# All of the squared-ReLU MLP's down projection as seven block products, with four moves around it

## The chip, the cores and the metric

The kernel runs on one core of a Trainium2 chip. The metric is the device time of one launch in microseconds (us), lower is better. TensorE (PE), VectorE (DVE), ScalarE (ACT), GpSimd (POOL) and SyncE (SP) run their own instruction streams and wait for each other by semaphores. SP issues nearly all loads, POOL most stores to scratch memory and every DMA that adds into its destination. Everything is in float32.

## What is computed

One layer of a streaming encoder, for 512 prompt frames and 32 sample frames taken together as T = 544 columns, with D = 2048:

```python
y, conv, k, v, logf = parallel_mixer(rmsnorm(x, g_mix), ...)      # gated conv ++ forgetting attention, w_in and w_out
x = x + y
x = x + cross_attention(rmsnorm(x, g_xattn), mk, mv, w_xq, w_xo)
x = x + square(relu(rmsnorm(x, g_mlp) @ w_up)) @ w_down           # hidden 8192
out = rmsnorm(x, g_final)
```

The gain of an RMS norm is put on the input of the projection that follows; the reciprocal root of the mean square (`rstd`) is a factor for each column, and is multiplied on the projection's output. So a projection's matmuls need not wait for the norm, but whatever takes its output does.

## The kernel before

**The arithmetic.** Activations lie transposed, a tile is 128 features x 544 columns (halves of TH = 272). A float32 operand is split into a rounded part and a rest: ACT copies it to `whi` (L84), DVE subtracts (`wlo`, L85), and a product takes three matmuls (hi·hi, hi·lo, lo·hi) of 128x128 weights by 272 columns. The large projections use a block scheme with seven products for a 2x2 block product instead of eight (class `Seven` for the input and up projections, with names b11, t1, t2, b22, t3, b21, t4): sums of weight blocks (`s1` to `s4`, tiles `sum`) and of activation blocks ("forms") are multiplied, and the results go to three PSUM areas (`mmx`, `mmy`, `mmz`). One "pair" is two output tiles, 7 products of 24 matmuls, 168 in all.

**The order.** The stages follow each other in program order: head (the first four input tiles, `w_first`), input projection by pairs, attention, output projection, cross-attention, its output projection with the residual tiles x3, up projection (32 pairs), down projection, final norm. A scheduler places each engine's instructions by the order in which they are written; `tc.high_priority(offset=AHEAD)` moves the splits and sums of weights ahead. Every engine then runs its own list in order: one that waits holds up all behind it.

**Buffers.** A pool tag with `bufs=n` is a ring: a tile waits until the one n before it is released. `raw` (3) and `raw2` (4 in the up projection) hold loaded weight blocks, `tmp` (6) holds passing tiles. Slots A, B, C of 16 tiles each hold the forms of the activations (t1/t2, b21/b22, t3/t4 in that order), later the down projection's forms 0 to 3 (A and B) and the residual x3 (C).

**Around the change.** The head sums the squares of x on DVE (`square`, L187), and `rb = rstd(acc_x, D, early=150)` is made before the first pair. The residual's squares go to `acc<-sq`, DMAs that add into two accumulators `acc_3` (L1085 to L1086); a chain of seven for each, each waiting for the one before. Their tiles `sq` are in the `raw2` ring except the last. The first up pair makes `rb_3` from them (matmuls `ssq`, L178), between t2 and b22.

The hidden layer has 64 tiles of 128. Tiles 4 to 59 (56 of 64) go as seven block products: 28 pairs leave `forms` in scratch memory (`fd`), and seven chunks of four pairs by eight output pairs p (L1251) run 7 products of 12 matmuls each. The first four and the last four tiles are plain: `hd`, `w_ends`, a stage of 384 matmuls (L1238) ahead of the chunks and another (L1327) behind them, the latter in two halves of columns, so that the first half's norm and the stores of its output (L1333) go beside the second half's matmuls. During the stage ahead SP loads the first chunk's forms.

Of the kernel before, what the change touches and what calls it, by code (L numbers as in the profile page):

```python
# [8 lines left out]
F32 = mybir.dt.float32  # L9
# [6 lines left out]
D = 2048  # L16
# [13 lines left out]
CH = 8  # L30
# [7 lines left out]
NF = 28  # L38
# [3 lines left out]
def hybrid_step(  # L42
# [3 lines left out]
    w_in, w_first, w_f, w_out, w_xq, w_xk, w_xv, w_xo, w_up, w_dn, w_ends,  # L46
# [9 lines left out]
    tpool = ctx.enter_context(tc.tile_pool(name="tmp", bufs=6))  # L56
# [111 lines left out]
    def rstd(acc, dim, width=T, early=0):  # L168
        accs = acc if isinstance(acc, list) else [acc]
        with tc.high_priority(offset=early):  # L170
            rt = npool.tile([128, T], F32, tag="rstd", name="rstd", bufs=3)
# [21 lines left out]
    wf = cpool.tile([128, KD, 8], F32, name="wf")  # L193
    wf_hl = cpool.tile([128, KD, 16], F32R, name="wf_hl")
# [128 lines left out]
    def seven(pl, ops, ws, out, scale, mid, prefetch, between=None, late=0):  # L323
# [12 lines left out]
        s.b22()  # L336
        s.t3()
# [13 lines left out]
    acc_x = new_acc()  # L351
# [3 lines left out]
    headp = head_cm.__enter__()  # L355
    heads = [mm_tile(), mm_tile()]
# [3 lines left out]
    for j in range(8):  # L360
        xr = [headp.tile([128, T], F32, tag="xr", name="xr", bufs=5) for i in range(2)]
        for i in range(2):
            sp.dma_start(xr[i], xT[j + 8 * i])
        hi, lo = weights(w_first[j])
        x = headp.tile([128, 4, TH], F32, tag="x", name="x", bufs=2)
        for i in range(2):
            act.activation(x[:, 2 * i:2 * i + 2], two(xr[i]), AF.Identity, scale=gain(G_MIX, j + 8 * i))
# [12 lines left out]
        for i in range(2):  # L380
            square(xr[i], acc_x, j + i == 0)
    head_cm.__exit__(None, None, None)
    act.dma_start(wf, w_f)
    split(wf_hl[:, :, 0:8], wf_hl[:, :, 8:16], wf)
# [14 lines left out]
    rb = rstd(acc_x, D, early=150)  # L399
    rbs = npool.tile([128, T], F32, tag="rstd", name="rbs", bufs=3)  # L400
    dve.tensor_scalar(rbs, rb, SCALE, None, ALU.mult)
# [151 lines left out]
    steps = (lambda: gate_open(z16), gate_exp, gate_log, gate_close, gate_sum, turn_logf)  # L553
    ps = emit_logf()
    nxt = fetch_pair(0)
    for t, (n, j) in enumerate((("hr", 0), ("gc", 0), ("gb", 0), ("hr", 1))):
        dve.tensor_tensor(first_tiles[t], first_tiles[t], rb, ALU.mult)
        kinds[n][1](j, first_tiles[t])
    z16 = evac_logf(ps)
    held = []  # L560

    def release():
        while held:
            held.pop()()

# [15 lines left out]
    for i in range(last):  # L581
# [3 lines left out]
        nxt = seven(pj, xops, nxt, out, scale, mid, ahead, release, 2 if i == 0 else 0)  # L585
        done(i, out[1])
        if i < len(steps):
            steps[i]()
        if pairs[i][1] == ("gb", 7):
            release()  # L590
# [833 lines left out]
```

## Time and profile before

| | |
|---|---|
| median of 3 runs | 2350.08 us (2349.14 to 2350.31) |
| profiled execution, its own time | 2352.74 us |
| its span | 2351.0 us (so 1.7 us lie around the span) |
| PE busy | 2312.8 us, 98%, 18151 matmuls |
| DVE busy | 1999.7 us, 85% |
| ACT / POOL busy | 1300.0 us, 55% / 212.2 us, 9% |
| DMA | 420.25 MB, mean 179 GB/s |

A matmul's record is longer (about 288 ns) than the distance to the next, since matmuls overlap; the pace is read from how many start in a stretch. In a row of the timeline, "x4" are records run together, and the bracket holds the idle time just before and what ended it. "PEclk" is the granted clock as a share of the full one.

### The profile page before, as it was taken

To read this page: it belongs to the slowest core of one execution; us is meant where nothing else is said; L and a number is where in the kernel's file an instruction comes from. 1 tells how busy PE (TensorE), PEld (TensorE's weight loads), DVE (VectorE), ACT (ScalarE), POOL (GpSimd) and SP (SyncE) were. 2 spreads that over 40 slices of the span, in tenths; PEclk is the share of its full clock that TensorE was granted. 3 is DMA by queue.
4 is the path that set the end of the run, shared out by engine and by line. 5 is a ranking of instruction groups with operands and counts; after the bars stand their busy time and mean duration, and the time that the engine had idled before them with its cause. 6 is when DMAs were issued, how large, how long until landed. Compare 5 with 4: busy or idle time off the path is not lost.

```text
span 2351.0 us, 47516 instructions
## 1 busy us (share of the span) xinstructions
PE 2312.8 (98%) x18151; PEld 2285.0 (97%) x18151; DVE 1999.7 (85%) x3546; ACT 1300.0 (55%) x2524; POOL 212.2 (9%) x402
## 2 busy tenths in 40 slices
PE   8999999999999999899999999999999999999997
PEld 8999999999999998799999999999999999999997
DVE  9999988877767757889999999998598888888887
ACT  8455555555644546556666566665255555555555
POOL 0000011114200001111111111111000000000000
PEclk9999999999999999999999999999999999999999
DMA  5333345578435537656565566556946636645523
GB/s 177 127 121 122 122 156 160 160 243 300 141 100 154 157 107 212 200 162 204 191 199 180 193 201 196 188 185 226 344 148 241 211 125 233 228 141 191 184 90 131
DMA packets 161861, 420.25 MB, mean 179 GB/s; under 512 B 19096, under 2 KB 23888, under 8 KB 161632
## 3 DMA queue, kind: packets, MB, share of 16 engines
q1 hardware_dynamic: 109888, 313.54, 39.8%
q0 software_dynamic: 46240, 94.75, 13.1%
q10 hardware_dynamic: 5504, 8.93, 1.1%
q8 instruction: 142, 2.33, 0.4%
q14 instruction: 87, 0.71, 0.1%
HBM read 319.91 MB, written 93.33 MB: 176 GB/s over the span
## 4 chain that ended last, share of the span: by engine, by line
PE 94%; DMA 2%; DVE 2%; ACT 1%; issue 1%; DVEq 0%; ACTq 0%; SPq 0%; POOLq 0%
PE mmx L271 27%; PE dx L1233 14%; PE mmy L271 14%; PE mm L120 13%; PE mm L1233 11%; PE mmz L271 7%; PE mm L1327 2%; PE mm L378 1%; PE h L378 1%; PE mm L914 1%; PE s L644 1%; DMA acc<-sq 1%; DMA raw<-in_w_ends 1%; DVE wlo L85 1%; DMA f<-fd 1%
## 5 line engine op out<-in xcount | busy, mean ns | idle before, releaser
L84 ACT ACTIVATE whi<-raw 128x512 fp32r<-128x512 f32 x664 | 417.8, 631 | 493.9 <-PE mmx L271 97.9
L84 ACT ACTIVATE whi<-sum 128x512 fp32r<-128x512 f32 x652 | 407.5, 630 | 418.6 <-PE mmx L271 186.2
L85 DVE TENSOR_TENSOR wlo<-raw,whi 128x512 fp32r<-128x512 f32 x664 | 453.3, 687 | 129.2 <-ACT whi L84 121.6
L85 DVE TENSOR_TENSOR wlo<-sum,whi 128x512 fp32r<-128x512 f32 x652 | 436.7, 684 | 70.3 <-ACT whi L84 65.9
L271 PE MATMUL mmx<-oph,whi 128*128 128x272 f32 x1296 | 372.8, 288 | 2.3 <-ACT h L280 2.2
L271 PE MATMUL mmx<-oph,wlo 128*128 128x272 f32 x1296 | 374.0, 289 | 0.1
L271 PE MATMUL mmx<-opl,whi 128*128 128x272 f32 x1296 | 371.5, 287 | 0.0
L1233 PE MATMUL dx<-f,whi 128*128 128x272 f32 x1792 | 344.4, 288 | 0.0
L1233 PEld LDWEIGHTS dx<-f,whi 128*128 128x128 f32 x1792 | 281.5, 188 | 0.0
L1233 PE MATMUL mm<-f,whi 128*128 128x272 f32 x1344 | 258.6, 288 | 0.0
L1233 PE MATMUL dx<-f,wlo 128*128 128x272 f32 x896 | 258.4, 288 | 0.0
L271 PE MATMUL mmy<-oph,whi 128*128 128x272 f32 x864 | 249.8, 289 | 7.6 <-ACT whi L84 7.6
L271 PE MATMUL mmy<-oph,wlo 128*128 128x272 f32 x864 | 249.9, 289 | 0.0
L271 PE MATMUL mmy<-opl,whi 128*128 128x272 f32 x864 | 248.9, 288 | 0.0
L271 PEld LDWEIGHTS mmx<-oph,whi 128*128 128x128 f32 x1296 | 244.0, 188 | 3.1 <-ACT h L280 2.6
L271 PEld LDWEIGHTS mmx<-oph,wlo 128*128 128x128 f32 x1296 | 243.3, 188 | 0.5 <-DVE wlo L85 0.5
L271 PEld LDWEIGHTS mmx<-opl,whi 128*128 128x128 f32 x1296 | 243.5, 188 | 0.0
L1233 PEld LDWEIGHTS mm<-f,whi 128*128 128x128 f32 x1344 | 210.6, 188 | 0.0
L1233 PE MATMUL mm<-f,wlo 128*128 128x272 f32 x672 | 193.4, 288 | 0.0
L271 PEld LDWEIGHTS mmy<-oph,whi 128*128 128x128 f32 x864 | 163.4, 189 | 8.1 <-ACT whi L84 8.0
L1233 PEld LDWEIGHTS dx<-f,wlo 128*128 128x128 f32 x896 | 168.9, 189 | 0.0
L271 PE MATMUL mmx<-b,whi 128*128 128x272 f32 x864 | 166.1, 289 | 0.1
(393 smaller groups left out, 5161.5 us busy)
## 6 DMA issues: line engine op xcount, KB each, us to landing
raw<-in_w_up SPq DMA_DIRECT2D x128, 512.0 KB, 3.9
raw<-in_w_dn SPq DMA_DIRECT2D x112, 512.0 KB, 4.4
f<-fd SPq DMA_DIRECT2D x196, 272.0 KB, 5.7
fd<-form POOLq DMA_DIRECT2D x168, 272.0 KB, 4.2
raw<-in_w_in SPq DMA_DIRECT2D x88, 512.0 KB, 3.8
raw<-in_w_out SPq DMA_DIRECT2D x32, 512.0 KB, 4.2
raw<-in_w_ends SPq DMA_DIRECT2D x20, 512.0 KB, 4.2
kq<-hl POOLq DMA_DIRECT2D x32, 256.0 KB, 3.3
```

The costliest lines, as they stand in the source:

```text
L84: act.activation(hi, src, AF.Copy)
L85: dve.tensor_tensor(lo, src, hi.bitcast(F32), ALU.subtract)
L120: pe.matmul(ps[a], w, two(x)[:, a], start=first and n == 0, stop=last and n == 2)
L271: pe.matmul(ps, a[:, c], x, start=first and j == 0 and n == 0, stop=j == 7 and n == 2, skip_group_check=not first)
L378: pe.matmul(ps[a], w[:, c], xs[a][q], start=j + i == 0 and n == 0, stop=j + i == 8 and n == 2)
L644: pe.matmul(s[:, :N], q[a][:, c], k[b][:, :N], start=n == 0, stop=n == 2)
L914: pe.matmul(ps[:, 0, :NMEM], w[:, c], x, start=k == 0 and n == 0, stop=k == KD - 1 and n == 2)
L1233: pe.matmul(ps, a[:, c], f[:, x], start=first and j == 0 and n == 0, stop=j == 3 and n == 2, skip_group_check=not first)
L1327: pe.matmul(ps, w[:, c], two(x)[:, a], start=k == 0 and j == 0, stop=k == 3 and j == 2)
```

## The change

1. All 64 hidden tiles go as block products: `NF` is 32 pairs instead of 28, the chunks are eight, `hd` and `w_ends` are gone. The last p of the last chunk is plain in two halves of columns, 96 matmuls (`ws`, `hs`; forms b12 of the last chunk are kept in `bd`); for it the final norm's squares go to POOL's adding DMAs (`complete`), and after it there are two `last_rstd`; the first half's eight stores follow the first of these.
2. The last two up pairs run in step (`fourteen`, product by product of both), and their forms are made in parts behind p = 1 to 6 of the first down chunk.
3. The first chunk's forms are loaded directly behind the last weights of the up projection, into slots A, B as they come free; new pools release their buffers tile by tile.
4. Residual's squares of j > 4 go to `tmp` (7 buffers instead of 6), and `rb_3` is written behind b22 (`behind`).
5. Head: the first weights are loaded ahead of x, its squares go to adding DMAs, and `rb`, its products with the first four tiles and their convolution move into the first input pair (`begin`). The pool `keep` closes later and a few sample tiles come from `tmp`.

```diff
-NF = 28
+NF = 4 * CH
-    tpool = ctx.enter_context(tc.tile_pool(name="tmp", bufs=6))
+    tpool = ctx.enter_context(tc.tile_pool(name="tmp", bufs=7))
...
-    def seven(pl, ops, ws, out, scale, mid, prefetch, between=None, late=0):
+    def seven(pl, ops, ws, out, scale, mid, prefetch, between=None, late=0, behind=None):
...
         s.b22()
+        if behind:
+            behind()
         s.t3()
...
+        if j == 0:
+            hi, lo = weights(w_first[j])
         for i in range(2):
             sp.dma_start(xr[i], xT[j + 8 * i])
-        hi, lo = weights(w_first[j])
+        if j:
+            hi, lo = weights(w_first[j])
...
         for i in range(2):
-            square(xr[i], acc_x, j + i == 0)
+            if j:
+                sq = tmp("sq")[:, :T]
+                act.activation(sq, xr[i], AF.Square)
+                pool.dma_start(acc_x[i], sq, accum_op=ALU.add)
+            else:
+                act.activation(acc_x[i], xr[i], AF.Square)
...
-    rb = rstd(acc_x, D, early=150)
...
+    def begin():
+        rstd(acc_x, D, out=rb)
+        for t, (n, j) in enumerate((("hr", 0), ("gc", 0), ("gb", 0), ("hr", 1))):
+            dve.tensor_tensor(first_tiles[t], first_tiles[t], rb, ALU.mult)
+            kinds[n][1](j, first_tiles[t])
+        box["z"] = evac_logf(ps)
+        dve.tensor_scalar(rbs, rb, SCALE, None, ALU.mult)
...
-        nxt = seven(pj, xops, nxt, out, scale, mid, ahead, release, 2 if i == 0 else 0)
+        nxt = seven(pj, xops, nxt, out, scale, mid, ahead, release if i else begin, 0 if i else 2)
...
-            sq = (tmp("sq") if j == 7 else up.tile([128, 1024], F32, tag="raw2", name="sq", bufs=4))[:, :T]
+            sq = (tmp("sq") if j > 4 else up.tile([128, 1024], F32, tag="raw2", name="sq", bufs=4))[:, :T]
...
-    for i in range(4 * CH):
+    for i in range(NF - 2):
         h1, h2 = tmp("h1")[:, :T], tmp("h2")[:, :T]
...
+        nxt = seven(up, ops, nxt, (h1, h2), (relu, relu), square_mid, ahead, None, 0 if i else 2,
+                    None if i else (lambda: rb_3.append(rstd(acc_3, D))))
+        square_mid(h2)
+        forms(i, h1, h2)
+    ss = [Seven(up, ops, ws, (tmp("h1")[:, :T], tmp("h2")[:, :T]), (relu, relu), square_mid, True) for ws in nxt]
+    fourteen(ss)
+    parts = []
+    for k, s in enumerate(ss):
+        square_mid(s.out[1])
+        parts += forms_in_parts(NF - 2 + k, *s.out)
...
+    fs = {f: load_form(0, f) for f in (5, 6, 0, 1)}
+    first = dweights(0, 0)
+    fs.update({f: load_form(0, f) for f in (2, 3)})
+    load_x3(0)
+    fs[4] = load_form(0, 4)
...
+        for p in range(8 if c < NF // 4 - 1 else 7):
...
+            if c == 0 and 1 <= p <= len(parts):
+                parts[p - 1]()
+            if c == NF // 4 - 1:
+                complete(p)
...
+            if a:
+                if i == 0:
+                    rb_4 = last_rstd(sums[0])
+                for p in range(4 * i, 4 * i + 4):
+                    store(p, 0, finish((0, p), rb_4, dve))
+    rb_4 = last_rstd(sums[1])
+    rb_5 = tmp("rb")[:, :TH]
+    act.activation(rb_5, rb_4, AF.Copy)
     for p in range(8):
-        store(p, 1, finish((1, p), rb_4))
+        store(p, 1, finish((1, p), rb_5 if p in (2, 4, 7) else rb_4, pool if p in (2, 4, 7) else dve))
```

What this does to the lists of instructions, at three places. PE in the first up pair, where the matmuls `ssq` of the residual's norm stand (`inv_88` is the matrix of 1/D; `mmx`, `mmy` with `b`, `oph`, `opl` are the pair's own products b11 and t1). Before, behind 23 matmuls of the pair:

```order
L271 MATMUL mmx<-b_12760,whi 128x272 x2
L271 MATMUL mmx<-b_12760,wlo 128x272
L271 MATMUL mmy<-oph,whi 128x272
L271 MATMUL mmy<-opl,whi 128x272
L178 MATMUL ssq<-acc,inv_88 128x272 x2
L271 MATMUL mmy<-oph,wlo 128x272
L271 MATMUL mmy<-oph,whi 128x272
```

And after:

```order
L269 MATMUL mmx<-b_12880,whi 128x272 x2
L269 MATMUL mmx<-b_12880,wlo 128x272
L269 MATMUL mmy<-oph,whi 128x272
L269 MATMUL mmy<-opl,whi 128x272
L269 MATMUL mmy<-oph,wlo 128x272
L178 MATMUL ssq<-acc,inv_88 128x272 x2
L269 MATMUL mmy<-oph,whi 128x272
L178 MATMUL ssq<-acc,inv_88 128x272 x2
L269 MATMUL mmy<-opl,whi 128x272
```

The first `ssq` moved from behind the pair's 23rd matmul to behind its 45th: still inside t1, and not behind b22, where it is written.

DVE in the first input pair, where the first tiles (`hr0`, `gc0`, `gb0`, `hr1`) take the norm's factor (`rstd_900` before, `rb_897` after). Before, between the sums and splits of the pair's first weights, ahead of the split of s2:

```order
L557 TENSOR_TENSOR hr0_888<-hr0_888,rstd_900 128x544
L85 TENSOR_TENSOR wlo_1153<-sum_1089,whi_1152 128x512
L557 TENSOR_TENSOR gc0_889<-gc0_889,rstd_900 128x544
L85 TENSOR_TENSOR wlo_1157<-sum_1089,whi_1156 128x512
L502 TENSOR_TENSOR u_1093<-gc0_889,hr0_888 128x512
```

And after, between the splits of a12 (`raw_1066`) and of a22 (`raw2_1064`), which is the pair's last product, t4:

```order
L85 TENSOR_TENSOR wlo_1299<-raw_1066,whi_1298 128x512
L579 TENSOR_TENSOR hr0_885<-hr0_885,rb_897 128x544
L579 TENSOR_TENSOR gc0_886<-gc0_886,rb_897 128x544
L579 TENSOR_TENSOR gb0_887<-gb0_887,rb_897 128x544
L514 TENSOR_TENSOR u_1201<-gc0_886,hr0_885 128x512
L515 TENSOR_TENSOR u_1201<-gc0_886,hr0_885 128x32
L579 TENSOR_TENSOR hr1_888<-hr1_888,rb_897 128x544
L518 COPY newc_976<-u_1201 128x2
L519 COPY newc_976<-u_1201 128x2
L522 TENSOR_SCALAR y_1208<-u_1201,vec_78 128x546
L582 TENSOR_SCALAR rbs_898<-rb_897 128x544
```

Here a run of unbroken work on the first tiles stands ahead of one split, where before it alternated with splits a pair earlier.

SP between the up and the down projection (`f` with `fd` are the chunk's forms, `x` with `x3d` the residual, `in_w_up`, `in_w_dn` and `in_w_ends` the weights). Before:

```order
L222 DMA raw<-in_w_up 128x1024
L93 DMA raw<-in_w_ends 128x1024 x2
L1193 DMA hh<-hd_0_11795 128x544
L1193 DMA hl<-hd_1_11796 128x544
L1193 DMA hh<-hd_0_11797 128x544
```

And after, from the last form 3 of the first chunk to the weights of p = 1:

```order
L1247 DMA f_21946<-fd_3_11822 128x544
L1247 DMA f_22097<-fd_0_11826 128x544
L1247 DMA f_22099<-fd_0_11833 128x544
L1247 DMA f_22101<-fd_0_11840 128x544
L1247 DMA f_21952<-fd_4_11802 128x544
L1247 DMA f_21954<-fd_4_11809 128x544
L1247 DMA f_21956<-fd_4_11816 128x544
L1282 DMA x_21948<-x3d_11778 128x544
L1282 DMA x_21950<-x3d_11779 128x544
L1247 DMA f_21958<-fd_4_11823 128x544
L1282 DMA x_21960<-x3d_11780 128x544
L1282 DMA x_21962<-x3d_11781 128x544
```

The plain stage's loads are gone. The 28 form tiles of the first chunk stand directly behind the up projection's weights, three forms of the second chunk among them, and the last form 4 stands behind two residual tiles that go to slots C.

More of the change, by code (lines that the diff above doesn't have):

```diff
@@ L1137, in hybrid_step @@
         xo_done(order[i], ps)
-    def plain(m, h):
-        f = ring("form")
-        hi, lo = (f[:, n].rearrange("p a b -> p (a b)") for n in range(2))
-        split(hi, lo, h)
-        pool.dma_start(hd[m][0], hi)
-        pool.dma_start(hd[m][1], lo)
     def forms(i, h1, h2):
@@ L1234, in dproduct, with load_x3 @@
                           skip_group_check=not first)
-    hs = load_hidden(0)
-    fs = [load_form(0, 0), load_form(0, 1)]
-    for p in range(8):
-        hi, lo = weights(w_ends[0, p])
+    def load_x3(p):
         for m in (2 * p, 2 * p + 1):
```

255 lines of the change are left out of this document (139 added, 116 removed).

## The prediction

> **What bounds the kernel now.** I read the page first: the shares of the engines, then the chain that ended last.
>
> ```profile
> span 2351.0 us, 47516 instructions
> PE 2312.8 (98%) x18151; PEld 2285.0 (97%) x18151; DVE 1999.7 (85%) x3546; ACT 1300.0 (55%) x2524; POOL 212.2 (9%) x402
> ...
> PE 94%; DMA 2%; DVE 2%; ACT 1%; issue 1%; DVEq 0%; ACTq 0%; SPq 0%; POOLq 0%
> ```
>
> PE is the bound nearly throughout; a change gains by fewer matmuls or by closing one of PE's few gaps, and loses where it makes another engine late. Next, stretches: near the start, around the first up pair, in the up projection, in the plain stage, in the chunks, in the last plain stage.
>
> ```profile
> core 0: us, PE busy (x) PEld busy (x) DVE busy (x) ACT busy (x) POOL busy (x), PEclk, DMA share, GB/s
> 60.00:100.00 40.00, 38.51 (x302) 34.99 (x300) 37.80 (x72) 17.04 (x34) 1.22 (x2) 1.00 0.35 121
> 100.00:300.00 200.00, 199.20 (x1586) 198.60 (x1586) 188.10 (x325) 103.50 (x187) 10.04 (x19) 1.00 0.37 121
> 955.00:976.00 21.00, 11.15 (x60) 9.41 (x58) 12.19 (x19) 8.17 (x16) 1.72 (x2) 0.76 0.78 221
> 960.00:970.00 10.00, 2.50 (x7) 1.83 (x7) 7.75 (x12) 3.33 (x6) 1.72 (x2) 0.59 0.86 230
> 1000.00:1600.00 600.00, 600.00 (x4785) 600.00 (x4785) 558.28 (x902) 365.16 (x679) 101.59 (x193) 1.00 0.59 191
> 1640.00:1660.00 20.00, 20.00 (x160) 19.99 (x160) 11.13 (x18) 6.30 (x12) 2.12 (x4) 1.00 1.05 361
> 1700.00:2280.00 580.00, 580.00 (x4623) 580.00 (x4623) 508.89 (x877) 306.31 (x606) 0.00 (x0) 1.00 0.53 181
> 2285.00:2336.00 51.00, 49.57 (x388) 48.59 (x386) 43.49 (x97) 37.56 (x85) 0.00 (x0) 1.00 0.41 135
> ```
>
> Steady stages have no gap: 600 us / 4785 matmuls = 0.1254 us each. DVE is at 93 to 94% in the pairs (558.28/600; 188.1/200), so what is added to it there has 6% of room. Only one stretch is bad: 21 us around 965 hold 60 matmuls where 168 fit. What PE waited for, in sums:
>
> ```profile
> PE mmy L271 <- ACT whi L84: 7.6, 2, 6.3
> PE mm L378 <- ACT whi L84: 7.1, 1, 7.1
> PE ssq L178 <- DMA acc<-sq: 3.4, 1, 3.4
> PE mmx L271 <- ACT h L280: 2.2, 2, 1.5
> PE mm L1327 <- DVE x L1329: 1.1, 1, 1.1
> ```
>
> The 7.1 are the kernel's start; 7.6 and 3.4 lie in the first up pair; the 1.1 lies in the last plain stage.
>
> **The change part by part.**
>
> *Matmuls.* Per output pair, seven products of 12 = 84 replace 96. Before: 384 + 384 + 7·8·84 = 5472 in the down projection. After: 63·84 + 96 = 5388. 84 fewer at 0.1254 us: **−10.5 us**, all on the path.
>
> *First up pair.*
>
> ```profile
> 955.04 0.41 PE L271 MATMUL mmx<-b,whi 128*128 128x272 f32 x2
> ...
> 964.15 0.60 PE L271 MATMUL mmy<-oph,whi 128*128 128x272 f32 x1 [6.30 <-ACT whi L84]
> ...
> 968.33 2.18 PE L178 MATMUL ssq<-acc,inv 128*128 128x272 f32 x4 [3.35 <-DMA acc<-sq]
> ...
> 970.76 0.43 PE L271 MATMUL mmy<-opl,whi 128*128 128x272 f32 x1
> 970.99 0.43 PE L271 MATMUL mmy<-oph,wlo 128*128 128x272 f32 x1
> ...
> 974.21 1.08 PE L178 MATMUL ssq<-acc,inv 128*128 128x272 f32 x4
> ...
> 977.17 0.39 PE L271 MATMUL mmy<-oph,whi 128*128 128x272 f32 x1 [1.27 <-ACT whi L84]
> ...
> 1646.33 0.42 PE L120 MATMUL mm<-hl,whi 128*128 128x272 f32 x2
> ```
>
> From 955.04 to 1646.33 are 691.3 us, against 32·168·0.1254 = 674.2 for the 32 pairs: the first one loses 17.1 (the later ones have no gap). Three waits are 10.9 of it, `ssq` 3.3, and the rest the slow pace after the idling: 0.23 us from one matmul to the next at 970.76, clock 0.59. The chain behind both waits is that of the adding DMAs:
>
> ```profile
> 952.09 0.86 POOL L1086 DMA_DIRECT2D acc<-sq  x1 [5.08 <-ACT sq L1085]
> ...
> 961.09 0.86 POOL L1086 DMA_DIRECT2D acc<-sq  x1 [6.13 <-DMA acc<-sq]
> 962.77 0.86 POOL L1086 DMA_DIRECT2D acc<-sq  x1 [0.82 <-DMA acc<-sq]
> ...
> DMA to landing us min/median/max: 4.0/6.7/8.2
> ```
>
> The squares hold `raw2` until their addition has landed, and the first pair's a21, a22 are loaded into that ring; so s1, its split and the 6.30 wait come out of it. With j > 4 in `tmp`, a21 and a22 wait only for j = 3's additions, and the 6.30 wait goes. What is late next is the accumulator itself: the last additions are issued at 961.09 and 962.77 and land some 7 us later, 968 to 970, whatever buffer they come from. In the order after, `ssq` stands behind 45 matmuls of the pair, so PE reaches it at 955.04 + 45·0.1254 = 960.7. Loss after: 960.7 to about 969.6 for wait and first `ssq` 8.9, second `ssq` 1.1, and some 4 us at 0.23 instead of 0.125, 1.8: 11.8. Gain 17.1 − 11.8 = **−5.3**. Bounds: no gain (chain 5 us later, since the weights now load beside it) and −12 (its last links take the 4.0 minimum).
>
> The Trainium skill, page "TensorE: Matmul & The Clock Gate", Part 1: The HAM clock gate, says that an idle window of about 3.4 us halves the clock and that about as much sustained work restores it. The rows agree (0.23 against 0.125 after 6.30 idle), and by it the wait that I leave in would again be followed by a half-rate stretch, as in my 1.8 us; were the wait under 3.4 us, that term would be nil.
>
> *Start.* The first weights now come ahead of x, and DVE scales the first x. Both rows needed for the first matmul (7.09) stay in the same chain of one load, a scaling and splits; bounds −0.7 and +0.8 (one ACT pass over 544 columns less or one more). I take **+0.4**, nearer the extra one, since ACT now copies two weights first. The DVE additions of x's squares (15 of about 0.64) leave the head, which PE bounds with 384 matmuls: nothing.
>
> *`begin`.* The rows of before:
>
> ```profile
> 66.34 0.71 DVE L557 TENSOR_TENSOR hr<-hr,rstd 128x544 f32<-128x544 f32 x1
> ...
> 75.80 0.78 DVE L88 SCALAR_TENSOR_TENSOR ych<-gb,vec,ych 128x544 fp32r<-128x544 f32 x1
> ...
> 77.48 2.48 DVE L85 TENSOR_TENSOR wlo<-sum,whi 128x512 fp32r<-128x512 f32 x4
> ```
>
> The first tiles' work stands between 66.34 and 77.48, 11.1 us, of which some 3.5 are splits and sums of weights: 7.6, and with rstd and rbs about 11 us of DVE. It is now late in the first pair, in an unbroken run of about 6 us ahead of a22's split. A product of 24 matmuls gives 3.0 us of cover, so t4 waits about 2.4 us, and the next pair's first splits about 1.4 twice; with the room of 6% DVE has caught up some 20 us later. Stalls of about 6 in place of those from 60 to 310 (1.5 at 77.45 among them, 3.3 to 4.3 in all): **+2.5**, bounds −1 (the wait at 77.45 gone, splits ahead in time) and +6 (no old stall saved). Four `ssq` in the pair instead of two at the head, at 0.54 (1.08 for two above): **+1.1**.
>
> *Up to down.* At 1640 to 1660 DMA moved 361 GB/s beside 384 plain matmuls (48 us): that cover is gone, and 28 form tiles of 272 KB, 7.6 MB, must land earlier. Slots A come free when t2 of the last two pairs ends, 24 us before the up projection does, slots B 12 us before; the 2.2 MB of each take 6 us at 361 GB/s. Form 4, x3 and the weights of p = 1 (2.3 MB more) compete at the boundary: stall 0 to 3. The forms in parts add about 1.6 us of DVE to p = 1 to 6, on 508.89/580, so 9.2 of the 10.5 that a p takes: a slight overload. Together **+1.5**, bounds 0 and +6 (two MB of 361 GB/s uncovered).
>
> *End.* The last stage runs from 2285 to 2335.7, 50.7 us for 384·0.1254 = 48.1; that 2.6 goes, and four `ssq` of the first half's norm come into the last 96 matmuls, 2.2: **−0.4**. Behind the last matmul:
>
> ```profile
> 2335.74 0.44 DVE L1329 TENSOR_TENSOR x<-x,mm 128x272 f32<-128x272 f32 x1
> ...
> 2337.23 0.72 PE L178 MATMUL ssq<-acc,inv 128*128 128x272 f32 x2 [1.53 <-DVE acc L163]
> ...
> 2340.74 5.17 DVE L1290 TENSOR_TENSOR yout<-yout,rstd 128x544 f32<-128x544 f32 x8
> ```
>
> 15.3 us to the end. After: five of the eight products on DVE (3.2 instead of 5.17, −2.0), one step less in the norm (−0.45), but the first half's products on DVE ahead of the last addition (four of 0.65, up to +2.6) and eight more stores at the very end, 2.2 MB that were spread over 24 us. **+0.5**, bounds −2 and +6 (those 2.2 MB at 361 GB/s). No row shows POOL in such a product. The Trainium skill, page "GPSIMD Engine Reference", section Elementwise — side-by-side cycle accounting, finds two-input elementwise work there about half as fast as on DVE; by that its three would take an estimated 3.9 us against DVE's 3.2 for five, about even.
>
> Sum: −10.5 − 5.3 + 0.4 + 2.5 + 1.1 + 1.5 − 0.4 + 0.5 = −10.2. The profiled execution's 2352.74 would be 2342.5; the median lies 2.66 below it, so **2340.0 us**.
>
> **The rivals.**
>
> *A. The chain of additions stays the whole loss.* The weights' loads move into 943 to 952, where the chain's last links run; DMA share is already 0.78 to 0.86. If each of the last two links lands 2 to 3 us later, the gain of 5.3 is gone: 2345.3, on the border of no change. For it: links took up to 8.2 under load. Against: the bytes are the same, only earlier.
>
> *B. The chain is quick.* Without raw2's block, additions could be issued as squares are made (last at 957), and with 4-us links land near 961: all but the `ssq` themselves and a little goes, −12 instead of −5.3: 2333. Against: POOL's rows at 961.09 wait for the previous addition, not for a buffer.
>
> *C. Slower: the down projection starts dry.* If the forms of the last two-pair stretch don't get through before the boundary (weights and six stored forms for each pair share the queues), 21 of 28 tiles, 5.8 MB, and 2.1 MB of weights come after it: 7.9 MB / 361 GB/s = 22 us, less the 3 to 10 that p = 0 covers: a stall of 12 to 19. It decides from 1.5 + 10.2 + 4.7 = 16 us of stall on; at 19, 2357. Against: the order has the loads directly behind the last weights, and slots A come free 24 us ahead.
>
> *D. DVE does not catch up.* At 94% load, a backlog of 6 us is worked off at 0.06 us per us only, 100 us, and every pair pays some of it: bounded by the backlog, +6 to +8 in place of +2.5: 2345.
>
> **How the numbers follow.** The forecast 0.52, A 0.16, B 0.13, D 0.10, C 0.09. A measurement can tell a change from none at about 0.2%, 4.7 us: below 2345.4 is faster, over 2354.8 slower. Faster: the forecast (0.50 of it), B, and some 0.08 each of A and 0.06 of D: 0.77. Slower: C's upper half and mishaps behind A, 0.06. The rest is the same, 0.17. The range reaches to B below, with the bounds of tail and start added (2329), and to A, D and half of C above (2350).
>
> **What would show it.** Right: 84 fewer down matmuls and chunks of 10.5 us each p; no wait for `whi` near 964, but one for the accumulator of 6 to 9 us at about 5.7 us into the first up pair, followed by matmuls 0.23 us apart; stalls on `wlo` in the first pair's t4; under 3 us of idle PE where up turns into down. Wrong: a wait over 10 us at that boundary, gaps that repeat pair by pair after 100 us, or more than 20 us from the last matmul to the end.

## The result and the profile after

The kernel became slower: 2367.29 us median of 4 runs (2366.63 to 2368.40) against 2350.19 (2349.14 to 2352.57, 4 runs) on the same chip, a ratio of 1.0068 [1.0056, 1.0081], 17 us. The forecast was 2340.0. The head of the page, then stretches as in the prediction (same columns): near the start, around the first up pair, the start of the down projection, its chunks, its last matmuls.

```profile
span 2364.9 us, 47573 instructions
PE 2310.9 (98%) x18083; PEld 2281.7 (96%) x18083; DVE 2008.1 (85%) x3562; ACT 1317.8 (56%) x2569; POOL 246.8 (10%) x447
```

```profile
60.00:100.00 40.00, 37.21 (x279) 34.42 (x280) 31.02 (x60) 15.63 (x31) 1.11 (x2) 0.96 0.30 102
950.00:960.00 10.00, 10.00 (x82) 10.00 (x82) 8.35 (x16) 5.95 (x11) 1.74 (x2) 1.00 1.05 318
960.00:970.00 10.00, 5.79 (x28) 5.25 (x27) 7.51 (x13) 7.38 (x13) 2.26 (x3) 0.66 1.03 309
1650.00:1740.00 90.00, 76.50 (x577) 75.40 (x576) 71.94 (x135) 42.35 (x90) 7.43 (x14) 0.96 0.71 249
1740.00:2280.00 540.00, 539.84 (x4304) 539.62 (x4303) 475.55 (x821) 288.30 (x572) 0.34 (x1) 1.00 0.56 193
2285.00:2347.00 62.00, 61.49 (x480) 60.51 (x479) 43.11 (x77) 41.12 (x87) 8.60 (x10) 1.00 0.41 97
```

PE executes 68 matmuls fewer: 84 products less, 16 `ssq` more (46 instead of 30). The chunks run without a gap (540 us / 4304 = 0.1255 us each). But 1650 to 1740, the first 90 us of the down projection, hold 577 matmuls where 90 / 0.1254 = 718 fit: some 17 us are lost there alone. The first up pair now begins 6 us later, at 960.86, and is still bad (28 matmuls in 960 to 970, before 7). From there to 1649.30 are 688.4 us, 14.3 more than the 674.2 that the prediction counts for 32 pairs.

Cut at four points that both traces have (the first `mm<-yah` of the output projection's second half, the first product of the down projection, its last plain matmul, the end of the span):

| stretch | before, us | after, us | change | foretold |
|---|---|---|---|---|
| start, input projection, attention | 692.79 | 698.79 | +6.0 | +4.0 |
| from there through the up projection | 952.54 | 950.51 | −2.0 | −5.3 |
| down projection to the last plain matmul | 690.09 | 697.53 | +7.4 | −9.4 |
| last plain matmul to the end | 15.6 | 18.1 | +2.5 | +0.5 |
| span | 2351.0 | 2364.9 | +13.9 | −10.2 |

What PE waited for after the change, in sums over the execution (total, times, longest):

```profile
PE mm L386 <- ACT b L84: 8.2, 1, 8.2
PE dx L1276 <- ACT e L1350: 7.9, 8, 3.3
PE dx L1276 <- ACT e L1360: 6.4, 2, 4.4
```

Rows two and three are new: the products of the down projection wait until ACT has copied an earlier product (`e`) out of PSUM. ACT is at 42.35 of 90 us there, so it isn't overloaded; something holds it. ACT's own waits in 1645 to 1735 name it, then a stretch of ACT's timeline, and PE's:

```profile
ACT fp L84 <- DMA fd<-fp: 19.4, 7, 6.0
```

```profile
1654.46 0.38 ACT L1355 ACTIVATE e<-dx 128x272 f32<-128x272 f32 x1
1660.78 0.43 ACT L84 ACTIVATE fp<-acc 128x272 fp32r<-128x272 f32 x1 [5.95 <-DMA fd<-fp]
...
1662.49 0.38 ACT L1360 ACTIVATE e<-dx 128x272 f32<-128x272 f32 x1
```

```profile
1662.92 0.82 PE L1276 MATMUL dx<-f,whi 128*128 128x272 f32 x2 [4.45 <-ACT e L1360]
...
1671.43 0.51 PE L1276 MATMUL dx<-f,whi 128*128 128x272 f32 x2 [2.23 <-ACT e L1350]
```

The forms in parts (`put` in `forms_in_parts`) take their tile `fp` from a ring of three. ACT's rounding copy into a fourth piece must wait until the store of the first has landed. The pieces are written behind p = 1 and later, but the scheduler placed them from the last up pairs on (the first copy starts at 1637.0). Around L1360 of p = 0 ACT's list, with its program names, reads

```
L1355 ACTIVATE e_21966<-dx 128x272
L84 ACTIVATE fp<-acc 128x272 x2
L1360 ACTIVATE e_21967<-dx 128x272
L84 ACTIVATE fp<-acc 128x272
L84 ACTIVATE whi<-raw 128x512
L84 ACTIVATE whi<-sum 128x512 x2
L84 ACTIVATE fp<-h_21400 128x272 x2
```

five pieces in nine instructions, and a ring of three. The first of them waits 5.95 us, the copy `e` at L1360 stands behind it on ACT, and PE, which needs the PSUM area that `e` empties, waits 4.45 and then goes at half rate (0.23 us from one matmul to the next until 1666). The stores themselves are slow there; the answer on the tile `fp` in 1635 to 1740 says

```profile
DMA to landing us min/median/max: 2.3/5.9/8.3
```

### The profile page after: what moved, and what is told of

Its sections match the earlier page's. It is cut to its first block, busy times and chain, and to the rows that moved or that the text cites. A ratio compares the mean times of both kernels' runs of the same rounds, so it can differ in the third digit from the quotient of the medians.

```text
span 2364.9 us, 47573 instructions
## 1 busy us (share of the span) xinstructions
PE 2310.9 (98%) x18083; PEld 2281.7 (96%) x18083; DVE 2008.1 (85%) x3562; ACT 1317.8 (56%) x2569; POOL 246.8 (10%) x447
## 5 line engine op out<-in xcount | busy, mean ns | idle before, releaser
L84 ACT ACTIVATE whi<-sum 128x512 fp32r<-128x512 f32 x676 | 422.4, 630 | 416.5 <-PE mmx L269 186.2
L85 DVE TENSOR_TENSOR wlo<-sum,whi 128x512 fp32r<-128x512 f32 x676 | 453.1, 686 | 88.1 <-ACT whi L84 85.3
L1276 PE MATMUL dx<-f,whi 128*128 128x272 f32 x2016 | 389.6, 289 | 14.3 <-ACT e L1350 7.9
L1276 PEld LDWEIGHTS dx<-f,whi 128*128 128x128 f32 x2016 | 317.6, 189 | 16.5 <-ACT e L1350 9.7
L1276 PE MATMUL mm<-f,whi 128*128 128x272 f32 x1512 | 292.1, 288 | 0.0
L1276 PE MATMUL dx<-f,wlo 128*128 128x272 f32 x1008 | 291.3, 289 | 0.0
L1276 PEld LDWEIGHTS mm<-f,whi 128*128 128x128 f32 x1512 | 238.2, 189 | 0.0
L1276 PE MATMUL mm<-f,wlo 128*128 128x272 f32 x756 | 218.1, 289 | 0.0
L1276 PEld LDWEIGHTS dx<-f,wlo 128*128 128x128 f32 x1008 | 190.6, 189 | 0.0
```

The source lines that it names most:

```text
L84: act.activation(hi, src, AF.Copy)
L85: dve.tensor_tensor(lo, src, hi.bitcast(F32), ALU.subtract)
L1276: pe.matmul(ps, a[:, c], f[:, x], start=first and j == 0 and n == 0, stop=j == 3 and n == 2, skip_group_check=not first)
```

## The experiments

Each kernel was timed against the kernel before on its own chip (medians; ratio with its 95% interval). The edits are against the changed kernel. Theory R is the ring just described; its rivals are that the pieces' work on ACT and DVE, or the traffic of forms, stores and weights at the boundary, is what PE waits for.

### The ring, without its stores

```diff
             split(two(f)[:, 0], two(f)[:, 1], x)
-            pool.dma_start(dst, f)
...
-            sp.dma_start(t.bitcast(F32), fd[4 * c + j][f].bitcast(F32))
+            i = 4 * c + j
+            sp.dma_start(t.bitcast(F32), fd[i if i < NF - 2 else i - 2][f].bitcast(F32))
```

> The changed kernel without the 16 stores of the forms that are made in parts (fp to fd and bd); the last chunk reads older pairs' forms in their place, so the output is not the reference's. The splits on ACT and DVE stay. Theory R (ring): ACT's copy into fp waits for one of 3 buffers that a store still holds (19.4 us of ACT idle on fd<-fp), the copies e of the down products stand behind it on ACT, and PE waits for them. Then the five PE gaps between 1655 and 1730 (13.5 us) and the half-rate stretches behind them go: from the last up matmul to the last plain matmul 697.7 becomes 678 to 681 us, time about 2348 to 2350. Theory W (work): 1.6 us of added DVE and ACT work for each p is too much; the work is unchanged, so the gaps stay within 2 us and the time is 2365 to 2367. Theory D (DMA): the loads of the second chunk saturate the queues and starve the first; only 4.4 MB of stores less, so at least 9 us of gaps stay, 2361 or more.

Measured: 2349.11 against 2351.18, 0.9995 [0.9986, 1.0005]. The down projection takes 680.43 instead of 697.53. The 90 us again:

```profile
1650.00:1740.00 90.00, 89.56 (x714) 89.34 (x713) 86.19 (x161) 52.04 (x107) 0.00 (x0) 1.00 0.73 261
```

714 matmuls instead of 577, with as many copies and subtractions, and no lower DMA share (0.73 against 0.71). So the work of the pieces isn't what PE pays for. The stores' own traffic is gone with them here; the next kernel keeps it.

### The same with every store kept

```diff
-            split(two(f)[:, 0], two(f)[:, 1], x)
+            hi, lo = two(f)[:, 0], two(f)[:, 1]
+            tc.keep_in_program_order(act.activation(hi, x, AF.Copy))
+            dve.tensor_tensor(lo, x, hi.bitcast(F32), ALU.subtract)
             pool.dma_start(dst, f)
...
+    def part(c, p):
+        if c + p and parts:
+            parts.pop(0)()
...
-            if c == 0 and 1 <= p <= len(parts):
-                parts[p - 1]()
+            part(c, p)
```

`part` is called at three places of each p, one piece at a time, and the copy may not be moved ahead of where it is written.

> The changed kernel, all stores kept, three buffers as before, but the 16 pieces of forms are written one at a time (two or three for each p from p = 1 on) and ACT's copy of each is pinned behind what is written ahead of it, so that no two of four wait in a row. Theory R: a piece needs its buffer only 13 us after the one before the last two, a store lands in 2 to 8, so ACT does not wait on fd<-fp; the gaps after the up projection go as without stores: last up matmul to last plain matmul 679 to 683 us (697.7), time 2348 to 2352. Theory W (added work): nothing gained, 2364 or more. Theory D (full queues after the boundary): the gaps of the first 30 us stay, 2358 to 2364.

Measured: 2350.89 against 2352.06, 0.9997 [0.9988, 1.0006]; down projection 680.42.

```profile
1650.00:1740.00 90.00, 89.83 (x715) 89.39 (x714) 86.79 (x163) 52.90 (x112) 8.52 (x16) 1.00 0.88 310
```

All 16 stores, more bytes (310 GB/s against 249) and a median landing of 4.5 us, and no stall: the stores were never too many, they were asked for too closely. This is the wait shown by itself, and 17.1 us of the down projection hang on it. Even without it the change as a whole can't be told from no change (0.9997): what the 84 matmuls save is lost again near the start and at the end.

### Half as many pieces

The last two pairs go one after the other; only the last pair's forms are made in parts.

```diff
-    for i in range(NF - 2):
+    for i in range(NF):
...
-        forms(i, h1, h2)
-    ss = [Seven(up, ops, ws, (tmp("h1")[:, :T], tmp("h2")[:, :T]), (relu, relu), square_mid, True) for ws in nxt]
-    fourteen(ss)
...
+        if i < NF - 1:
+            forms(i, h1, h2)
+    parts = forms_in_parts(NF - 1, h1, h2)
```

> The changed kernel with the last two up pairs one after the other (not in step); pair 30's forms are made at once as for all others, only pair 31's in parts (8 stores instead of 16). Theory R: half of the ring's waits stay, so the gaps after the up projection shrink from 13.5 to 4 to 7 us; slots A are free 12 us instead of 24 us before the up projection ends, which still holds 6 us of loads: boundary stall 0 to 3. Time 2354 to 2359. Theory W: half of the loss too, gaps near 7. Rival S (the step is needed): loads of forms 0 to 3 come late, over 6 us of PE waiting for forms in the first 10 us of the down projection, time over 2362.

Measured: 2370.33 against 2351.18, 1.0083 [1.0068, 1.0098]: a miss. Eight pieces are still bunched at the boundary, and the blocked instruction is now also a split of weights:

```profile
1657.89 0.43 ACT L84 ACTIVATE fp<-h 128x272 fp32r<-128x272 f32 x1 [4.59 <-DMA fd<-fp]
```

```profile
PE mm L1272 <- ACT whi L84: 8.0, 2, 6.1
```

Halving the pieces is thus no cure while more than three still come close together, with ACT's urgent work behind them. It is no clean test of their number either: without the step the loads at the boundary come later too, DMA is at 1.07 from 1650 to 1690, and a store lands after 6.5 us in the median instead of 5.9.

### The old head

All of item 5 undone: x before the weights, squares of x on DVE, `rb` and the first tiles ahead of the first pair.

```diff
-            if j:
-                sq = tmp("sq")[:, :T]
-                act.activation(sq, xr[i], AF.Square)
-                pool.dma_start(acc_x[i], sq, accum_op=ALU.add)
-            else:
-                act.activation(acc_x[i], xr[i], AF.Square)
+            square(xr[i], acc_x, j + i == 0)
...
+    rb = rstd(acc_x, D, early=150)
...
-        nxt = seven(pj, xops, nxt, out, scale, mid, ahead, release if i else begin, 0 if i else 2)
+        nxt = seven(pj, xops, nxt, out, scale, mid, ahead, release, 0 if i else 2)
```

> The changed kernel with the head of before: x ahead of the first weights, squares of x added on DVE, rstd before the first pair, the first tiles' products and convolution beside the first pair's first splits (wf_hl in a passing tile instead of a constant one). Theory B: the 6.0 us that the changed kernel is behind when attention starts (698.8 against 692.8) come from the start (+1.1) and from begin's DVE run ahead of a22's split with the backlog after it; all of it goes: attention's first output matmul at 693 +- 1, time about 2361. Rival: the backlog is from something else in the input projection (tmp ring, later exit of keep): less than 2 us come back, 2365 or more.

Measured: 2359.85 against 2351.18, 1.0037 [1.0022, 1.0052], 7.4 us less than the changed kernel (its four runs lie between 2356.7 and 2362.4). The first stretch takes 691.72 instead of 698.79, and from 60 to 100 us PE has

```profile
60.00:100.00 40.00, 38.86 (x304) 35.26 (x302) 38.16 (x72) 17.08 (x35) 1.30 (x2) 1.00 0.37 126
```

304 matmuls instead of 279. DVE is busier (38.16 against 31.02) and PE nonetheless faster: freeing DVE bought nothing here. The difference lies from 80 to 200 us: 951 matmuls start there in all five traces with the old head (the kernel before and those at the end among them), 896 to 901 in all eight with the new one.

### `begin` early, the rest of the new head kept

```diff
+    begin()
+
     def job(i):
...
-        nxt = seven(pj, xops, nxt, out, scale, mid, ahead, release if i else begin, 0 if i else 2)
+        nxt = seven(pj, xops, nxt, out, scale, mid, ahead, release, 0 if i else 2)
```

> The changed kernel with the same head (first weights ahead of x, squares of x by adding DMAs), but begin (rb, the first tiles' products and convolution) ahead of the first pair, as before the change, instead of between t2 and b22. Theory B1 (the late place of begin costs): without its unbroken DVE run ahead of a22's split the stalls at 92.9 (2.6), 101.6 (1.2) and 191.4 (0.9) go; attention starts 2 to 4 us earlier (695 to 697 against 698.8), time 2363 to 2365; what PE pays is a wait for the last adding DMAs at the head's end, 1 to 3 us. Theory B2 (the adding DMAs cost, begin's late place only hides them): PE waits 4 us or more at ssq at the head's end, attention at 698 or later, no gain or slower.

Measured: 2369.41 against 2351.26, 1.0079 [1.0065, 1.0093], and the first stretch takes 700.71, no less than 698.79. B2's time came true, but not its place: PE doesn't wait at `ssq`. One later wait carries the loss, and the 40 us hold 248 matmuls:

```profile
PE mmx L269 <- ACT h L278: 6.4, 1, 6.4
```

```profile
60.00:100.00 40.00, 33.57 (x248) 30.95 (x247) 30.70 (x56) 14.08 (x27) 1.11 (x2) 0.91 0.28 95
```

So an early `begin` is no cure: the norm itself comes late. DVE's first product with `rb` starts at 73.86 us here, against 66.34 in the kernel before. What costs is the new head as a whole. Which of its parts (adding DMAs instead of DVE, two accumulators and so four `ssq`, or the weights ahead of x) has which share was not taken apart further.

### The residual's squares: other ways

Back in `raw2` (all but j = 7):

```diff
-            sq = (tmp("sq") if j > 4 else up.tile([128, 1024], F32, tag="raw2", name="sq", bufs=4))[:, :T]
+            sq = (tmp("sq") if j == 7 else up.tile([128, 1024], F32, tag="raw2", name="sq", bufs=4))[:, :T]
```

> The changed kernel with the residual's squares of j = 5 and 6 back in raw2 (as before the change; 7 tmp buffers and rb_3 behind b22 kept). Theory A: the wait only changes its place between raw2 (weights a21, a22 late) and tmp (residual's reloads late); up projection with its start 688 to 691 us as in both, time 2366 to 2370. Rival 1 (part 4 did help): over 693 us, 2371 or more. Rival 2 (tmp costs more than raw2 did): under 686 us, 2364 or less.

Measured: 2369.42 against 2352.06, 1.0073 [1.0058, 1.0088]. PE's waits from 940 to 1000 are the old ones again:

```profile
PE mmy L269 <- ACT whi L84: 6.3, 2, 5.1
PE ssq L178 <- DMA acc<-sq: 3.3, 1, 3.3
```

Against the changed kernel that is some 2 us, but the two intervals overlap. In the trace, the stretch through the up projection takes 953.8 us against 950.5; five more kernels with the squares as in the change take 950.8 to 953.5. So that the step helps at all isn't shown. In the changed kernel itself, ACT, then PE around the first up pair, then the loads of weights and of the residual in 940 to 975 (times, KB each, median us from issue to landing):

```profile
960.15 0.66 ACT L1102 ACTIVATE sq<-x2r 128x544 f32<-128x544 f32 x1 [3.36 <-issue]
```

```profile
964.12 0.59 PE L269 MATMUL mmy<-oph,whi 128*128 128x272 f32 x1 [3.10 <-ACT whi L84]
...
973.29 1.08 PE L178 MATMUL ssq<-acc,inv 128*128 128x272 f32 x4
```

```profile
raw<-in_w_up SPq DMA_DIRECT2D x6, 512.0 KB, 8.6
...
x2r<-x2d SPq DMA_DIRECT2D x3, 272.0 KB, 8.5
```

`ssq` starts without a wait, so the accumulator is not what is late. In these rows the residual is: the squares now occupy `tmp`, from which `x2r`, the residual's reload, also takes its tiles, and both it and the weights land 8.5 us after their issue, with DMA at 1.05 and 1.03 in 950 to 970 (before the change the same two lines say 5.3 and 5.1). ACT's square at 960.15 starts 3.36 us late, and the profile names no releaser. By the order in which `tmp` (seven tiles) is taken, it needs the tile of a residual whose store was issued at 953.55; that this store is what it waits for is worked out from the kernel, not shown by a run.

Without any adding DMA: PE sums the squares, 32 more matmuls of a rounded copy, whose tiles all come from `tmp`.

```diff
-            sq = (tmp("sq") if j > 4 else up.tile([128, 1024], F32, tag="raw2", name="sq", bufs=4))[:, :T]
...
-            pool.dma_start(acc_3[i], sq, accum_op=ALU.add)
+        sq = tpool.tile([128, T + 4], F32R, tag="t", name="sq")[:, :T]
...
+        for a in range(2):
+            pe.matmul(ssq_3[a], inv_r, two(sq)[:, a], start=i + j == 0, stop=i + j == 8)
```

> The changed kernel with the residual's squares summed on PE: each square tile is written rounded to fp32r and multiplied with a matrix of 1/D into two PSUM areas as it is made, 32 matmuls of 0.125 us (4.0 us) in place of 14 adding DMAs and 8 records ssq (2.2 us). Theory A (the chain of adding DMAs is what is late, by its length, and by the tmp buffers that it keeps from the residual's reloads): the first up pair loses 3 to 7 us instead of 15, PE pays 1.8 more, time 2357 to 2361. Rival (the weights' loads under full queues are what is late): the wait for a21 and a22's sum stays, loss over 11, time 2365 to 2369.

Measured: 2364.52 against 2352.06, 1.0055 [1.0038, 1.0072]: 2.8 us less than the changed kernel, against 6 to 10 expected, with intervals that overlap; its stretch through the up projection takes 951.8 us, no less than 950.5. The traffic is gone, and the two lines of loads say 3.9 and 2.9 us, but look at 950 to 980 in its trace:

```profile
950.00:960.00 10.00, 10.00 (x82) 10.00 (x81) 9.68 (x18) 9.23 (x17) 0.00 (x0) 1.00 0.72 237
960.00:970.00 10.00, 9.74 (x79) 9.52 (x77) 8.61 (x15) 7.76 (x14) 0.00 (x0) 1.00 0.23 86
970.00:980.00 10.00, 6.55 (x35) 5.72 (x34) 9.11 (x14) 5.93 (x13) 0.00 (x0) 0.78 0.25 73
```

DVE (9.68 of 10, third pair of numbers) is now what is late; the hole moves to 970 to 980, with 35 matmuls, and 32 matmuls more are paid. So neither the chain of additions nor the late loads were the only limit of this stretch.

On GpSimd instead of by DMA:

```diff
-            pool.dma_start(acc_3[i], sq, accum_op=ALU.add)
+            pool.tensor_tensor(acc_3[i], acc_3[i], sq, ALU.add)
```

> The changed kernel with the residual's squares added by GpSimd's own tensor_tensor into acc_3 instead of by adding DMAs; 14 additions, 1.3 us each by the three products on GpSimd in the tail (3.92 us for 3). Theory A: the chain of adding DMAs (3.6 to 8.1 us a link) holds the squares' tiles, now in tmp, and the residual's reloads (x2r, in tmp too) wait for them: ACT idle at 956.8 to 960.2, additions of x2r at 965.3 and 967.8. Without the chain the first up pair loses 4 to 6 us instead of 15, time about 2357. Rival: PE waits for the loads of a21 and a22 under full DMA queues, whatever the squares do: loss stays at 12 or more, 2364 to 2367. Rival: GpSimd's work slows DVE by more than 5 us there.

Measured: 2374.05 against 2351.18, 1.0101 [1.0084, 1.0117]: worse by 7. DVE and POOL around 930 us:

```profile
929.11 0.43 DVE L206 TENSOR_TENSOR ts<-x,ts 128x272 f32<-128x272 f32 x1
...
930.09 1.60 DVE L209 TENSOR_TENSOR ts<-x,ts 128x272 f32<-128x272 f32 x1
```

```profile
930.02 1.38 POOL L1103 TENSOR_TENSOR acc<-acc,sq 128x544 f32<-128x544 f32 x1 [2.05 <-ACT sq L1102]
```

The same kind of DVE instruction takes 0.43 alone and 1.60 when it starts with POOL's addition. The Trainium skill, page "GPSIMD Engine Reference", section Specifications, says that its SBUF interface is shared with VectorE and that instructions with two SBUF inputs contend; the row agrees, and gives the size: 1.2 us of DVE for 1.4 us of POOL. In a stage where PE waits for DVE's additions that is paid: from 900 to 1000 us PE waits seven times, 5.3 us in all, for the additions `x2r` (L1095), and the stretch through the up projection takes 959.4 us.

### Putting the parts together

Old head and pieces one at a time, once with PE's squares (first kernel), once with the new end below (second), once with both (third). The end is a rearranged `store`: the first half's products follow the last addition, every second one on POOL, and POOL takes p = 5 and 7 of the second half.

```diff
-                for p in range(4 * i, 4 * i + 4):
-                    store(p, 0, finish((0, p), rb_4, dve))
+                    rb_5 = tmp("rb")[:, :TH]
+                    act.activation(rb_5, rb_4, AF.Copy)
+                else:
+                    for p in range(8):
+                        store(p, 0, finish((0, p), rb_5 if p % 2 else rb_4, pool if p % 2 else dve))
```

> The changed kernel with three of the experiments together: head of before, pieces of forms spread and pinned, squares of the residual on PE. If the three causes are separate, the gains add: 7.4 for the head as measured, 16 to 19 for the pieces, 6 to 10 for the squares: 2331 to 2338, 12 to 19 us faster than the kernel before. If the gaps only move (a later wait takes over), 2342 or more.

Measured: 2344.03 against 2352.06, 0.9967 [0.9954, 0.9980]. It missed its 2331 to 2338 because PE's squares, which it counted on, gave next to nothing: 2367.3 less 7.4 for the head and 16.4 for the pieces is 2343.5.

> The changed kernel with the pieces spread and pinned, the head of before, and a changed end: the first half's eight products are all behind the last additions, odd ones on GpSimd (1.3 us each, 5.2 for four) beside DVE (0.65), the second half's on DVE but for two. The squares of the residual stay as the change has them. Head and pieces alone: 2367.3 - 7.4 - 16.4 = 2343.5. If the end is bound by DVE (DVE busy without a gap from 2344.7 to 2357.4 in the changed kernel), the stretch from the last matmul of the down projection to the end shrinks from 18.1 to 15.5 to 16.5: 2341 to 2343. If it is bound by the 16 stores at about 0.7 us each behind the norm, it stays at 17.5 or more: 2343 to 2345.

Measured: 2343.71 against 2351.26, 0.9965 [0.9951, 0.9978], in the range that it gives for an end bound by the stores.

> The same with the residual's squares summed on PE. PE pays 4.0 - 2.2 us and gains 3 us of waits in the first up pair, as the trace without adding DMAs showed (3.7 us of waits for splits and a half-rate stretch left): within 2 us of the kernel without it, 2340 to 2345. If the half-rate stretch behind the two waits of 1.5 us is by chance absent, 2 us less.

Measured: 2341.98 against 2351.26, 0.9959 [0.9947, 0.9972]. That is 9.3 us less than before. The intervals of the three overlap, so which of them is best is not settled.

The tail, last plain matmul to the end, is 17.4 and 17.65 us in the last two, 18.1 in the changed kernel. There DVE's list shows what stands ahead of the last addition:

```profile
2346.57 2.62 DVE L1293 TENSOR_TENSOR yout<-yout,r 128x544 f32<-128x544 f32 x4
2349.10 0.43 DVE L1392 TENSOR_TENSOR x<-x,mm 128x272 f32<-128x272 f32 x1
...
2354.18 3.25 DVE L1293 TENSOR_TENSOR yout<-yout,r 128x544 f32<-128x544 f32 x5 [0.46 <-ACT rb L1404]
```

The addition waits behind four of the first half's products and comes 2 us after its matmul. Moving them behind it gained 0.7 us. In the second kernel the second half's products still start 7.15 us behind the last plain matmul, against 7.35 (before the change 5.3), because ACT and DVE now wait elsewhere: ACT's `r` stands behind the first half's stores, which ACT issues and which wait for their products, and DVE's `q` takes 1.02 us beside POOL's products (0.43 in the changed kernel):

```profile
2328.62 0.49 ACT L1282 ACTIVATE r<-ssq,eps 128x272 f32<-128x272 f32 x1 [1.47 <-DVE yout L1273]
```

```profile
2329.60 1.02 DVE L1285 TENSOR_TENSOR q<-r 128x272 f32<-128x272 f32 x1
```

From the second half's first product to the end it takes 10.3 us in the second kernel, 10.7 in the changed one and 10.3 before the change, where DVE did all eight. There the stores are the limit (6 of the second kernel's last 8.3 us):

```profile
2334.00:2337.00 3.00, 0.00 (x0) 0.00 (x0) 1.92 (x4) 0.00 (x0) 0.72 (x1) 0.50 1.04 352
2337.00:2340.00 3.00, 0.00 (x0) 0.00 (x0) 0.00 (x0) 0.00 (x0) 0.00 (x0) 0.50 1.03 354
```

The second half's eight stores, 2.2 MB, take an estimated 6.3 us at 354 GB/s, more than eight products on DVE (5.17 us before the change). All 16 output tiles, 4.5 MB, now leave behind the last matmuls, an estimated 12.6 us at that rate, however the products are dealt out.

## Why the prediction was wrong, point by point

**The matmuls** (−10.5) were right. With the ring's waits out, the down projection takes 680.4 instead of 690.1, 9.7 less; for matmuls and last stage together −10.9 was foretold. The missing 1.2 lies within what the last chunk and stage lose: from 2285 to 2347 PE has 480 matmuls, 60.2 us in 62.

**Up to down** (+1.5) is the step that failed: 17.1 were lost. I wrote that "The forms in parts add about 1.6 us of DVE to p = 1 to 6" and priced them by busy time on DVE. The price was on ACT, which had more than half its time free: a copy that waits for a buffer holds everything behind it, whatever the engine's load, and the buffer comes free only when a store has landed, 5.9 us in the median. Three buffers, four or more pieces in a row, and an engine on which PE's next product depends would have been enough to see it; the list quoted above could be read before any run. The sign that I had named, a wait over 10 us, isn't what it looks like: there are five waits, the longest 4.45. Rival C put the loss at the right place, at 12 to 19 us, but for another reason: its forms arrive in time, as the kernel with all stores spread shows (310 GB/s in the same 90 us, no stall). The size would have fitted and the theory was wrong.

**Start and `begin`** (+4.0 in three terms) came to +6.0, and 7.1 against the old head in the changed kernel. The stall that I foretold ahead of a22's split, 2.4 us, is there:

```profile
92.88 0.60 PE L269 MATMUL mmx<-oph,wlo 128*128 128x272 f32 x1 [2.28 <-DVE wlo L85]
```

The half rate behind it (0.23 us from one matmul to the next until 96) is not what the prediction lacked. In six other kernels with this head the same wait, 2.27 to 2.28 us, is not followed by it, and 80 to 200 us hold as few matmuls: 896 here, 55 or 6.9 us fewer than before. I had stalls of about 6 there, so their size was near; but I took 3.3 to 4.3 of old stalls off, and the kernel before has only six matmuls less than fit in these 120 us, 0.7 us. My reason, the late place, is not the whole of it: moved early, `begin` costs as much. Nor is it the first matmul, which comes at 8.24 instead of 7.09: the kernel with the old head whose first matmul comes at 8.23 has 389 matmuls by 60 us, as many as the kernel before. Which part of the new head makes the norm late stays open.

**The first up pair** (−5.3) brought −2.0 in these two traces. Of the difference 1.0 is a row that I misread: at 1646.33 the plain stage had been running for 1.0 us (its first matmul is at 1645.33), so the first pair lost 16.1, against 14.3 now, and the sum gives −4.3. The wait of t1 on `whi` did not go; it shrank from 6.30 to 3.10 and now stands at the very start of the pair (964.12). The sum of a21 and a22 no longer waits for its load, as foretold, but for its turn on DVE, behind a row that waits for ACT. Before, then after:

```profile
962.15 1.23 DVE L232 TENSOR_TENSOR sum<-raw,raw 128x1024 f32<-128x1024 f32 x1 [5.76 <-DMA raw<-in_w_up]
```

```profile
961.48 0.73 DVE L205 TENSOR_TENSOR ts<-x 128x544 f32<-128x544 f32 x1 [3.13 <-ACT x L1106]
962.12 1.22 DVE L230 TENSOR_TENSOR sum<-raw,raw 128x1024 f32<-128x1024 f32 x1
```

"What is late next is the accumulator itself" was wrong: `ssq` waits for nothing, and by the rows the next late thing was the residual. That removing its traffic gained little, with DVE busy throughout, the kernel with PE's squares shows. Rival A was right that most of the gain goes, not in its reason: the chain's last ten links landed after 3.6 to 8.1 us, no later than the 4.0 to 8.2 before.

**The tail** (+0.5) came to +2.5, inside its bounds of −2 and +6. The products ahead of the last addition cost 2 us, as foretold ("up to +2.6"). The term that failed is the −2.0 for dealing the second half's products out: from their start to the end it takes 10.7 us, no less than the 10.3 before, since the stores behind them set that time.

**DVE does not catch up** (rival D): it did. From 100 to 300 us two waits are left, 0.93 at 101.59 and 0.63 at 191.43, and the last 100 us of it hold 799 matmuls, all that fit.

The errors are 15.6, 2.0, 3.3 and 2.0 by term, and 1.2 for the matmuls: 24.1 from −10.2 to +13.9. The moved work was priced by how busy its engine is, and no rival asked what it holds up behind it, which is why none of them held the cause.

## What to carry to other kernels

Price a moved piece of work by how long it holds its buffers and by what stands behind it on its engine, not by its share of busy time: count the pieces that stand in a row, the buffers in the ring, and the time until each is released, here 5.9 us for a store against 0.43 us of work. Taking a wait out of one ring by moving its tiles to another can make the second ring's other users late; ask who else takes from it. Spread such pieces one at a time and pin them where they are written: here the scheduler pulled the first of them forward into the up projection, to 1637.0. And before a step is made faster, ask what runs behind it: faster products gained nothing while the stores took longer.

## What the hardware showed that I had not expected

A half-rate stretch came after an idle time of 2.28 us (at 92.88 above; the granted clock is 0.50 from 94 to 96), but not after 2.23 (at 1671.43), and not after the same wait at the same place in six other kernels, such as the one with all stores spread (granted clock 1.00 from 92 to 96):

```profile
92.44 0.40 PE L269 MATMUL mmx<-oph,wlo 128*128 128x272 f32 x1 [2.27 <-DVE wlo L85]
```

In the kernel with PE's squares it came after 1.64:

```profile
973.60 0.39 PE L271 MATMUL mmx<-oph,whi 128*128 128x272 f32 x1 [1.55 <-ACT whi L84]
...
976.01 0.59 PE L271 MATMUL mmy<-oph,whi 128*128 128x272 f32 x1 [1.64 <-ACT whi L84]
976.40 0.43 PE L271 MATMUL mmy<-opl,whi 128*128 128x272 f32 x1
```

Between the two gaps stand four matmuls. So it isn't the length of one gap that decides: two short ones, close together, were enough here, and one of 2.28 us had either outcome. After the 3.10 us at 964.12 half rate came too (0.23 us from one matmul to the next until 970), where the prediction, by the Trainium skill, would have had none under 3.4 us. The Trainium skill, page "TensorE: Matmul & The Clock Gate", Part 1: The HAM clock gate, gives an idle window of about 3.4 us and says that the window runs freely; the rows agree with a window that starts on its own, not with a gap that must itself last 3.4 us. That a window mostly idle (1.55, four matmuls, 1.64) is enough fits the rows, but no run here tests it.

A landing time is no constant: stores of 272 KB to scratch memory took 2.3 to 8.3 us in one stretch of 100 us. And POOL's products at the very end, three of 1.31 us, left DVE's five at 0.65 each beside them, unlike its additions around 930; at the end DVE's second operand lies in PSUM. DVE's `q` above, which reads SBUF alone, took 1.02 us instead of 0.43 beside such products. That the place of the operand is the reason was not tested by itself.
